# One projection unit moved among the indexer's products, and the search's first logits placed two units later

## Chip, cores and metric

The kernel runs on one core of a Trainium2 chip. The metric is the device time of one execution in microseconds (us). The engines are called PE (matrix products), DVE (vector), ACT (activation), POOL (GpSimd) and SP (the queue that issues nearly all DMAs here).

## What is computed

One layer over 2048 tokens of width 1024: a root-mean-square norm, one wide projection, two attention branches with gates, an output projection, and a last norm.

```python
xn = rms_norm(h, norm_gain[layer])
proj = xn @ w_in[layer]
qa, ka, va, ga, qb, kb, vb, gb, iq, ik, iw, za, zb = jnp.split(proj, offsets, axis=-1)
ya = chunked_relpos_attention(qa, ka, va, rel_bias[layer]) * jax.nn.silu(ga)
...
yb = dsa_sparse_attention(qb, kb, vb, iq, ik, iw) * jax.nn.silu(gb)
gate_a = jax.nn.sigmoid(za + b_merge[layer, 0])
gate_b = jax.nn.sigmoid(zb + b_merge[layer, 1])
merged = gate_a * (ya @ w_branch_a[layer]) + gate_b * (yb @ w_branch_b[layer])
h = h + merged @ w_out[layer]
```

`dsa_sparse_attention` first scores all admissible keys of a query with the small indexer (`iq`, `ik`, `iw`: eight heads of width 32), keeps the best 256, and attends to those only.

## The kernel before

Tokens are worked on in four groups of 512. Every fp32 product is done as three products of rounded halves (`mm3`, L212): high by high, high by low, low by high. A product of 128 output columns with one group is thus 24 matmuls of 128x512 (8 slices of the width by 3), into one PSUM bank.

**Stage 1, the indexer.** The groups come in the order 2, 3, 0, 1 (index `i` from 0 to 3). Each has three products of 128 columns, `chain(i, m)`. The columns hold the indexer's queries, its keys, its head weights, and the key of branch B. For the first two groups the norm's factor is applied after the product; for the last two (groups 0 and 1) `scaled(i)` applies it before: DVE multiplies eight slices in place (L230), ACT writes the high half `xh` (L231), DVE the low half `xl` (L232). The factor comes from `squares(i)` (sums of squares of rows, on ACT), `root_columns` (a chain of tiny DVE operations) and `root_rows` (four PE transposes into the bank `trr`, then an ACT copy, L305). `evac_i(i, m)` empties a bank: for `m = 0` through the rotary tables `cs` (loaded by DMA into one buffer) into `ea`; then ACT and DVE write a high and a low half into `e` (three buffers, L337 and L338) and SP sends them to DRAM as `iqD`, `ikD` and `kB`. After the second and the fourth group the keys come back in another layout as `ikT` (L348). `weights_t` transposes the head weights (`trw`).

**Stage 2, the projection.** The other columns stand in 20 units of 256 columns (`UNITS`; unit 0 is the first quarter of `zb`). `prep(u)` loads a unit's weights through staging tiles `wst` (SP), and splits them: ACT the high half (L209), POOL the low half (L210). There are two weight buffers `wt`. In stage 1 they hold the inputs `xw` and the indexer's weights `w01`, so that unit 0 can be prepared only when group 0 has been scaled, and unit 1 only when the last indexer product is done. The list `jobs` goes through the units, first for groups 0 and 1 (two jobs a unit, two products a job), later for groups 2 and 3. `evac` empties a bank; for `zb` ACT applies the sigmoid with the bias `bm` and SP stores the tile in `sBD`.

**The search** runs beside stage 2. `tick(x)` stands behind each product and calls `pump`, which takes as much work as `PUMP * x` allows from two threads: `logits()` (the indexer's scores, `lg`: eight matmuls for each piece of keys, from `iqT` and `ikT`) and `search()` (the thresholds, on DVE and ACT). From the 142nd tick on, when both threads have ended, the same ticks start stage 3, the attention.

The code's order is not the engines' order: a scheduler places each engine's instructions, in PE's queue too, by times of its own. Within an engine and within SP's queue the order is then fixed, and an instruction that waits holds up all behind it.

The lines on which the change and the prediction rest are these (the numbering of the profile).

Of the kernel before, what the change touches and what calls it, by code (L numbers as in the profile page):

```python
# [8 lines left out]
F32 = mybir.dt.float32  # L9
# [87 lines left out]
def block_kernel(ctx: ExitStack, tc: tile.TileContext, io, dbg=None):  # L97
# [91 lines left out]
    wcur = {}  # L189
    stage = [(wpool, 2, 2)]  # L190

    def prep(u, gate=None, at=None):
        if (at or u) in wcur:
            return
        wt = wpool.tile([128, 2, KT, WT], F32R, name="wt", tag="wt")
        if UNITS[u][0] == "va":
            st = stage[-1][0].tile([128, KT, 32], F32, name="wst", tag="wst", bufs=stage[-1][2])
            nc.sync.dma_start(st, io["wV"][UNITS[u][1]])
            nc.scalar.activation(wt[:, 0, :, 256:288], st, AF.Copy)
            nc.gpsimd.tensor_tensor(wt[:, 1, :, 256:288], st, f32(wt[:, 0, :, 256:288]), op=OP.subtract)  # L200
        for c in range(2):
            pl, n, bufs = stage[-1]
            for k in range(0, KT, n):
                st = pl.tile([128, n, 128], F32, name="wst", tag="wst", bufs=bufs)
                if gate is not None:
                    nc.gpsimd.tensor_copy(st[:, 0, 0:1], gate)
                nc.sync.dma_start(st, io["wP"][u, c, :, k:k + n, :])
                hi = wt[:, 0, k:k + n, c * 128:(c + 1) * 128]
                nc.scalar.activation(hi, st, AF.Copy)  # L209
                nc.gpsimd.tensor_tensor(wt[:, 1, k:k + n, c * 128:(c + 1) * 128], st, f32(hi), op=OP.subtract)  # L210
        wcur[at or u] = wt
# [22 lines left out]
    with ExitStack() as ph:  # L234
# [59 lines left out]
        def root_columns(i, n):  # L294
            v = xp.tile([128, 4 * n], F32, name="v4", tag=f"v{n}{i}")
            nc.vector.tensor_scalar(v, ss[:, 4 * i:4 * i + 4 * n], 1.0 / D, EPS, op0=OP.mult, op1=OP.add)
            r = rsqrt(xp, v, f"rs{n}{i}", 4 * n)
            for z in range(n):
                inv_[i + z] = r[:, 4 * z:4 * z + 4]

        def root_rows(i):
            tr = psl.tile([128, 512], F32, name="trr", tag="lg1")
            for j in range(4):
                nc.tensor.transpose(tr[:, j * 128:j * 128 + 128], inv_[i][:, j:j + 1].to_broadcast([128, 128]), ident)
            nc.scalar.activation(roots_[order[i]], tr, AF.Copy)  # L305
# [3 lines left out]
        def chain(i, m, c=all_):  # L309
            s_ = SLOT[order[i]]  # L310
            if (i, m) not in accs:
                n = rot("first", 7)
                accs[i, m] = (psp, psp, ps, ps, ps, psl, psl)[n].tile([128, 512], F32, name="xa",
                                                                       tag=f"acc{n}" if n < 5 else ("lg0", "ptr0")[n - 5])
            w_ = w_of(m)
            mm3(accs[i, m][:, c], [((w_[0][:, k], w_[1][:, k]), (xh[s_][:, k, c], xl[s_][:, k, c])) for k in range(KT)])
# [38 lines left out]
            nc.scalar.activation(iw[:, 4 * g:4 * g + 4, :], tr[:, :, 112:120], AF.Copy, scale=0.0625)  # L355

        nc.sync.dma_start(gcol, io["g1"])
        for k in range(0, KT, 2):
            load_x(0, k, k + 2, halves[0])
            load_w(0, k)  # L360
# [8 lines left out]
        def scaled(i):  # L369
            for k in range(KT):  # L370
                split_x(SLOT[order[i]], k, x32[i % 2][:, k], roots_[order[i]])

        def roots_of(i):
            root_columns(i, 1)
            root_rows(i)
# [18 lines left out]
        for m in range(3):  # L394
            chain(1, m)
        scaled(2)
        for m in range(3):
            evac_i(0, m)
        weights_t(0)
        for m in range(3):  # L400
            chain(2, m)
        squares(3)
        roots_of(3)
        squares(1)
        roots_of(1)
        scaled(3)
        prep(0)
        for m in range(3):
            evac_i(1, m)
        weights_t(1)  # L410
        for m in range(3):
            evac_i(2, m)
        for m in range(3):
            chain(3, m)
# [1 line left out]
        for m in range(3):  # L416
            evac_i(3, m)
        weights_t(3)


    ph = phase_p
    evl = search_st.enter_context(pool("evl", bufs=2, side="right"))
# [210 lines left out]
        nc.vector.tensor_scalar(gt, gt, -1.0, -FAR, op0=OP.add, op1=OP.mult)  # L633
        nc.gpsimd.dma_start(mskD[b, :, :n], gt)

    nc.sync.dma_start(bm, io["bm"])
    threads = {0: logits(), 1: search()}
    clock = {0: 0.0, 1: 0.0}

# [538 lines left out]

    def tick(x):
        due[1] += x  # L1180
        if threads:
            pump(PUMP * x)
        elif due[1] > OPEN:
            if not early_:
                open_early()
            due[0] += x * ROUNDS
            while due[0] >= 1 and not paused:
                due[0] -= 1
                if next(att_gen) == "late":
                    paused.append(1)  # L1190
# [13 lines left out]
    def next_acc(i):  # L1204
        n = rot("acc", 3 if 1 < i < ACC3 else 2)
        return (psp, psp, psz)[n].tile([128, 512], F32, name="acc", tag=f"acc{n}")
# [83 lines left out]
    for i, (how, r_, u, g) in enumerate(jobs):  # L1290
        kind, c2 = UNITS[u]
        wt, s_ = wcur[r_], SLOT[g]
        if how == "one":
            for n, _ in enumerate(first_half(u, wt)):
                if u == quads[-1] and n == 1:
                    for k in range(4):
                        combine_pe(A21, A22, A21, 1, k, 1)
                tick(0.5)
        for c in range(0 if how == "one" else 4 if kind == "va" else 2):
            acc = next_acc(i)  # L1300
            if kind == "va":
                c_ = slice(c * 128, c * 128 + 128)
                mm3(acc[:, :WT], [((xh[s_][:, k, c_], xl[s_][:, k, c_]), (wt[:, 0, k, :], wt[:, 1, k, :]))
                                  for k in range(KT)])
                evac_v(c2, g, c, acc[:, :WT])
                for _ in range(1):
                    if again:
                        again.pop(0)()
                tick(0.5)
            else:  # L1310
                w_ = slice(c * 128, c * 128 + 128)
                mm3(acc, [((wt[:, 0, k, w_], wt[:, 1, k, w_]), (xh[s_][:, k, :], xl[s_][:, k, :]))
                          for k in range(KT)])
                evac(kind, c2 * 2 + c, g, acc)
                for _ in range(2):
                    if again:
                        again.pop(0)()
                tick(1)
        if i in range(BI0, BI0 + 16):
            bias_half(i - BI0, f32(wt[:, 1, KT - 1, 255:256]))  # L1320
        if (u, g) in ((b_, 0), (b_, 1)) and r_ < nu:
            again += norm_again(g + 2)
        if i == turned:
            again += [lambda k=k: combine(A21, A11, A21, OP.subtract, k) for k in range(4)]
        for n in after.get(i, []):
            if n < nu:
                prep(n)
            elif n < 2 * nu:
                prep(n - nu, at=n)
            else:  # L1330
                while again:
                    again.pop(0)()
                prep_one(n - 2 * nu, n)
# [204 lines left out]
```

## Time and profile before

| what | value |
|---|---|
| median of three runs | 2072.44 us (2071.0 to 2077.87) |
| the profiled execution, its own time | 2072.23 us |
| its span, first to last instruction | 2070.4 us |
| PE busy | 1988.5 us, 96% of the span |
| DVE, ACT, POOL busy | 71%, 61%, 39% |
| mean granted PE clock | 0.991 |

A row of the timeline gives the start, the length, the engine, the line and the tiles (out<-in), the number of instructions merged, and in brackets how long the engine had been idle and what released it. Matmuls overlap, so a row's length is more than the distance to the next one. In the table of windows, each stretch has its length, each engine's busy time with the number of instructions, the granted PE clock and the DMA engines' share. Stage 1 reaches to about 100 us, stage 2 to about 1016 us.

### The profile page before, as it was taken

How to read it: one execution, taken by the hardware profiler on the slowest of the kernel's cores; microseconds unless marked ns; L12 is line 12 of the kernel's file. 1: busy time of each engine (PE TensorE's matmuls, PEld its weight loads, DVE VectorE, ACT ScalarE, POOL GpSimd, SP SyncE). 2: the span in 40 equal slices, each digit the busy share in tenths (PEclk: the TensorE clock that was granted, in tenths of full speed). 3: DMA queues.
4: the chain of work that ended last, by engine and by line, in shares of the span. 5: the costliest groups of instructions: out<-in, count | busy, mean ns of one | idle time of the engine just before them, and what ended most of it. 6: DMA issues, size and time to landing. Idle time of an engine off the chain costs nothing.

```text
span 2070.4 us, 34079 instructions
## 1 busy us (share of the span) xinstructions
PE 1988.5 (96%) x10674; PEld 1684.4 (81%) x10674; DVE 1472.0 (71%) x3646; ACT 1266.2 (61%) x2484; POOL 798.6 (39%) x1043
## 2 busy tenths in 40 slices
PE   8799999999999999999898999999999999999998
PEld 7588887889889887877677889888888888887786
DVE  6748887978789987474466768758886688765444
ACT  5456566556567554244587869858987688773221
POOL 2122233321132454444345464454444633432410
PEclk9899999999999999999999999999999999999999
DMA  9473345464464665578999775565355631335642
GB/s 359 143 236 129 120 133 161 129 207 143 172 193 138 217 212 188 186 238 286 285 308 275 210 234 153 169 221 160 120 168 166 219 114 52 99 94 179 214 137 92
DMA packets 262154, 375.75 MB, mean 181 GB/s; under 512 B 32080, under 2 KB 127696, under 8 KB 261840
## 3 DMA queue, kind: packets, MB, share of 16 engines
q1 hardware_dynamic: 261968, 373.53, 56.6%
q8 instruction: 85, 1.39, 0.3%
q14 instruction: 101, 0.83, 0.1%
HBM read 252.88 MB, written 120.55 MB: 180 GB/s over the span
## 4 chain that ended last, share of the span: by engine, by line
PE 43%; DMA 5%; DVE 3%; ACT 3%; issue 3%; POOL 2%; SPq 1%; DVEq 0%; POOLq 0%; ACTq 0%
PE d L218 7%; PE acc L218 6%; PE po L1433 6%; PE O L1016 5%; PE s L991 5%; PE pt L1008 4%; PE O L926 3%; PE s L881 2%; PE pt L916 2%; DMA mf<-mD 1%; DMA wst<-wS 1%; DVE P L812 1%; ACT P L994 1%; POOL dw L1055 1%; DMA bias<-biasD 0%
## 5 line engine op out<-in xcount | busy, mean ns | idle before, releaser
L218 PE MATMUL acc<-xh,wt 128*128 128x512 f32 x2160 | 696.8, 396 | 17.6 <-ACT wt L1250 7.8
L218 PEld LDWEIGHTS acc<-xh,wt 128*128 128x128 f32 x2160 | 405.3, 189 | 114.6 <-ACT wt L1250 11.0
L218 PE MATMUL acc<-xl,wt 128*128 128x512 f32 x1080 | 424.1, 393 | 0.0
L833 POOL TENSOR_TENSOR ptl<-pf,pth 128x512 fp32r<-128x512 f32 (+1 forms) x144 | 180.1, 1251 | 229.7 <-ACT pf L829 158.6
L218 PEld LDWEIGHTS acc<-xl,wt 128*128 128x128 f32 x1080 | 203.9, 189 | 43.0
L210 POOL TENSOR_TENSOR wt<-wst,wt 128x512 fp32r<-128x512 f32 (+1 forms) x92 | 118.2, 1312 | 271.5 <-ACT wt L209 239.6
L836 DVE TENSOR_TENSOR ptl<-pt,pth 128x512 fp32r<-128x512 f32 (+1 forms) x288 | 187.9, 660 | 43.6 <-ACT pth L835 42.0
L487 DVE SCALAR_TENSOR_TENSOR sc<-lg,iw,sc 128x512 f32<-128x512 f32 (+2 forms) x266 | 178.9, 679 | 42.4 <-ACT lg L482 37.2
L991 PE MATMUL s<-kBt,qsB 128*128 128x512 f32 (+3 forms) x640 | 187.1, 384 | 2.4 <-DVE mx L812 2.1
L482 ACT ACTIVATE lg<-lg 128x512 f32<-128x512 f32 (+2 forms) x304 | 149.4, 523 | 63.3 <-PE lg L480 61.9
L835 ACT ACTIVATE pth<-pt 128x512 fp32r<-128x512 f32 (+1 forms) x288 | 159.8, 579 | 26.2 <-PE pt L1008 16.0
L1008 PE MATMUL pt<-ident,P 128*128 128x128 f32 x1088 | 166.6, 273 | 1.0 <-DVE ptl L836 0.6
L994 ACT ACTIVATE P<-P,mx 128x128 f32<-128x128 f32 (+15 forms) x128 | 154.8, 1210 | 18.7 <-DVE mx L812 18.5
L1016 PE MATMUL O<-ptl,vBt 128*128 128x256 f32 x544 | 148.7, 299 | 2.7 <-POOL ptl L833 1.5
L1016 PE MATMUL O<-pth,vBt 128*128 128x256 f32 x544 | 147.6, 289 | 2.1 <-ACT pth L835 0.7
L812 DVE CUSTOM_DVE_ANT_0 P<-s,mk,mx 128x512 f32<-128x512 f32 (+2 forms) x192 | 125.2, 652 | 32.5 <-PE s L991 26.3
L1008 PEld LDWEIGHTS pt<-ident,P 128*128 128x128 f32 x1088 | 127.7, 140 | 9.0 <-DVE ptl L836 1.8
L1250 ACT ACTIVATE wt<-wst 128x512 fp32r<-128x512 f32 (+1 forms) x144 | 75.1, 570 | 86.7 <-POOL wst L1350 43.7
L1055 POOL TENSOR_TENSOR dw<-dst,dw 128x512 fp32r<-128x512 f32 x64 | 82.5, 1291 | 94.1 <-ACT dw L1054 86.8
L1251 DVE TENSOR_TENSOR wt<-wst,wt 128x512 fp32r<-128x512 f32 (+1 forms) x144 | 92.6, 675 | 32.6 <-ACT wt L1250 32.3
L991 PEld LDWEIGHTS s<-kBt,qsB 128*128 128x128 f32 x640 | 102.2, 190 | 14.9 <-DVE mx L812 8.1
L881 PE MATMUL s<-kk,qs 128*128 128x320 f32 (+1 forms) x448 | 107.0, 335 | 7.2 <-DVE mx L812 3.5
(274 smaller groups left out, 4442.2 us busy)
## 6 DMA issues: line engine op xcount, KB each, us to landing
wst<-wP SPq DMA_DIRECT2D x84, 256.0 KB
wst<-wS SPq DMA_DIRECT2D x72, 256.0 KB
qs<-qA SPq DMA_DIRECT2D x128, 128.0 KB
kk<-kA SPq DMA_DIRECT2D x56, 256.0 KB
vs<-vA SPq DMA_DIRECT2D x56, 256.0 KB
qD<-q SPq DMA_DIRECT2D x54, 256.0 KB
wst<-wS SPq DMA_DIRECT2D x72, 192.0 KB
part<-qD SPq DMA_DIRECT2D x54, 256.0 KB
```

What stands on the lines that cost most here:

```text
L218: nc.tensor.matmul(acc, a, b, start=(first and i == 0), stop=(last and i == n - 1), **({} if first and last else {"skip_group_check": True}))
L482: nc.scalar.activation(lg, lg, AF.Relu)
L487: nc.vector.scalar_tensor_tensor(o_, lg, wv, o_, op0=OP.mult, op1=OP.add)
L812: nc.vector.tensor_tensor_reduce(dst, ps_, add, 1.0, FMAX if first else mx, OP.add, OP.min, accum_out=mx)
L833: nc.gpsimd.tensor_tensor(lo, pf, f32(hi), op=OP.subtract)
L835: nc.scalar.activation(hi, src, AF.Copy)
L836: nc.vector.tensor_tensor(lo, src, f32(hi), op=OP.subtract)
L881: nc.tensor.matmul(s_ps[:, :w], q[:, m, j * 128:(j + 1) * 128], kk[:, ko:ko + w], start=(m == 0), stop=(m == 1))
L991: nc.tensor.matmul(s_ps[:, :w], q[:, h, :], kBt[:, m, a:a + w], start=(m == 0), stop=(m == 1))
L994: nc.scalar.activation(P[:, e, :n], P[:, e, :n], AF.Exp, bias=mx[:, e:e + 1], scale=-1.0, accum_out=st["sum"][:, (u % 2) * 2 + e:(u % 2) * ...
L1008: nc.tensor.transpose(pt[:, k, e, :], P[:, e, (kt + k) * 128:(kt + k + 1) * 128], ident)
L1016: nc.tensor.matmul(o_, vBt[:, kt + k, :], src[:, k, :], start=(kt + k == 0 and n_ == 0), stop=(kt + k == b and n_ == 1), skip_group_check= ...
```

## The change

Unit 0 for group 0 (two products, 48 matmuls) is taken out of the list of jobs and written into stage 1, with its own evacuation. Its weights are loaded right after group 0 is scaled, through the staging tiles of stage 1 (six buffers of 128 KB, in place of two), and its bias table `bm` at the very start. Group 0's products are written in another order, one of them is evacuated at once, and the counter that hands out banks skips one. The job that is left empty still ticks twice, and `tick` does nothing until its count is over 4, so that the first logits come after the fifth product's tick, where they came after the first's.

```diff
+    def prep(u, gate=None, at=None, via=None):
...
+            pl, n, bufs = via or stage[-1]
...
+                st = pl.tile([128, n, 128], F32, name="wst", tag="wis" if via else "wst", bufs=bufs)
...
         nc.sync.dma_start(gcol, io["g1"])
+        nc.sync.dma_start(bm, io["bm"])
...
         scaled(2)
+        prep(0, via=(xp, 2, 6))
         for m in range(3):
             evac_i(0, m)
         weights_t(0)
-        for m in range(3):
-            chain(2, m)
         squares(3)
-        roots_of(3)
+        root_columns(3, 1)
+        chain(2, 1)
+        chain(2, 0)
+        root_rows(3)
+        chain(2, 2)
+        evac_i(2, 1)
+        scaled(3)
+        for c in range(2):
+            acc = (ps, psl)[c].tile([128, 512], F32, name="xa", tag=("acc2", "ptr0")[c])
+            c_ = slice(c * 128, c * 128 + 128)
+            mm3(acc, [((wcur[0][:, 0, k, c_], wcur[0][:, 1, k, c_]), (xh[0][:, k], xl[0][:, k])) for k in range(KT)])
+            e = ev.tile([128, 512], F32, name="ef", tag="ef")
+            nc.scalar.activation(e, acc, AF.Sigmoid, bias=bm[:, 8 + c:9 + c])
+            nc.sync.dma_start(sBD[0][c_], e)
+        rot("first", 7)
         squares(1)
         roots_of(1)
-        scaled(3)
-        prep(0)
...
-        for m in range(3):
+        for m in (0, 2):
             evac_i(2, m)
...
-    nc.sync.dma_start(bm, io["bm"])
...
     def tick(x):
         due[1] += x
+        if due[1] <= 4:
+            return
...
+            if i == 0:
+                tick(1)
+                continue
```

Three places show how the scheduler places this. First, PE in stage 1, where the root factors of groups 3 and 1 are transposed (`rs13y`, `rs11y` belong to indices 3 and 1); `xh_142` to `xl_145` are group 0's halves, `xh_146` to `xl_149` those of the next group, `w_181` and `w_182` the indexer's weights, `wt` those of unit 0. Before:

```order
L218 MATMUL xa<-xh_144,w_181 128x512
L304 MATMUL trr<-ident,rs13y 128x128 x4
L304 MATMUL trr<-ident,rs11y 128x128 x4
L218 MATMUL xa<-xh_146,w_181 128x512
L218 MATMUL xa<-xh_146,w_182 128x512
```

Now:

```order
L218 MATMUL xa<-xh_144,w_181 128x512
L304 MATMUL trr<-ident,rs13y 128x128 x4
L218 MATMUL xa<-xh_142,wt 128x512 x2
L218 MATMUL xa<-xl_143,wt 128x512
L218 MATMUL xa<-xh_142,wt 128x512 x2
L218 MATMUL xa<-xl_143,wt 128x512
```

Between the two sets of transposes there now stand 43 of the 48 matmuls of unit 0 (the other five come 24 matmuls earlier), and behind them the transposes of `rs11y` and the last group's products.

Second, SP's queue from the last group's writes to the weights of unit 1 (`wst`). Before:

```order
L344 DMA ikD<-e 8x2x512
L344 DMA iqD<-e 32x2x512 x2
L344 DMA kB<-e 8x2x512 x2
L348 DMA ikT<-ikD 32x1024 x4
L344 DMA iqD<-e 128x2x512
L344 DMA iqD<-e 32x2x512 x2
L344 DMA kB<-e 48x2x512
L457 DMA iqT<-iqD 32x8x128 x4
L698 DMA sBD_94<-ef 128x512
L457 DMA iqT<-iqD 32x8x128 x4
L698 DMA sBD_94<-ef 128x512
L207 DMA wst<-wP 128x512 x5
```

Now:

```order
L708 DMA sBD_95<-ef 128x512
L344 DMA ikD<-e 24x2x512
L344 DMA ikD<-e 8x2x512
L344 DMA iqD<-e 32x2x512 x2
L344 DMA kB<-e 8x2x512 x2
L348 DMA ikT<-ikD 32x1024 x4
L344 DMA iqD<-e 128x2x512
L344 DMA iqD<-e 32x2x512 x2
L344 DMA kB<-e 48x2x512
L708 DMA sBD_95<-ef 128x512
L468 DMA iqT<-iqD 32x8x128 x2
L207 DMA wst<-wP 128x512 x5
```

Four loads of `iqT` went ahead of the last group's writes and two behind the weights; a store of the sigmoid's result (`sBD`, of unit 0 with group 1) now stands ahead of those writes.

Third, PE around the first logits (`lg`). Before, they stand inside the last product of unit 0:

```order
L218 MATMUL acc<-xh_146,wt 128x512
L218 MATMUL acc<-xl_147,wt 128x512
L218 MATMUL acc<-xh_146,wt 128x512 x2
L480 MATMUL lg<-ikT,iqT 128x384 x5
L218 MATMUL acc<-xl_147,wt 128x512
```

Now they stand between unit 0's last product and unit 1's first, all eight in a row:

```order
L354 MATMUL trw<-ident,ea 128x128 x4
L218 MATMUL acc<-xh_148,wt 128x512 x2
L218 MATMUL acc<-xl_149,wt 128x512
L218 MATMUL acc<-xh_148,wt 128x512
L491 MATMUL lg<-ikT,iqT 128x384 x8
L218 MATMUL acc<-xh_142,wt 128x512
L218 MATMUL acc<-xl_143,wt 128x512
```

The last 5294 of PE's 10676 instructions, from about 1172 us in the run before (the first products of branch B's output), stand in the same order in both kernels.

More of the change, by code (lines that the diff above doesn't have):

```diff
@@ L190, in block_kernel @@
     stage = [(wpool, 2, 2)]
-    def prep(u, gate=None, at=None):
+    def prep(u, gate=None, at=None, via=None):
         if (at or u) in wcur:
@@ L201, in prep @@
         for c in range(2):
-            pl, n, bufs = stage[-1]
+            pl, n, bufs = via or stage[-1]
             for k in range(0, KT, n):
-                st = pl.tile([128, n, 128], F32, name="wst", tag="wst", bufs=bufs)
+                st = pl.tile([128, n, 128], F32, name="wst", tag="wis" if via else "wst", bufs=bufs)
                 if gate is not None:
```

## The prediction, made before the changed kernel ran

> **What bounds the kernel now.** I read the page's busy times and slices first, then the table of windows, then PE's timeline for the first 130 us, since all that the change moves lies there.
>
> ```profile
> PE 1988.5 (96%) x10674; PEld 1684.4 (81%) x10674; DVE 1472.0 (71%) x3646; ACT 1266.2 (61%) x2484; POOL 798.6 (39%) x1043
> PE   8799999999999999999898999999999999999998
> ```
>
> PE is the bound: it is idle for 82 us of 2070.4, and the slices put much of it in the first two (52 us each). Both kernels give PE the same 10,676 matmuls, so a gain can only come from PE's idle time or its clock.
>
> ```profile
> 50.00:66.00 16.00, 12.85 (x61) 10.23 (x60) 11.43 (x39) 10.24 (x21) 4.55 (x5) 1.00 0.60 205
> 66.00:70.00 4.00, 0.98 (x5) 0.70 (x5) 2.67 (x6) 2.37 (x5) 2.18 (x3) 0.84 0.72 200
> 70.00:78.00 8.00, 1.05 (x2) 0.29 (x1) 7.97 (x9) 5.02 (x9) 4.10 (x3) 0.50 0.02 4
> 78.00:84.00 6.00, 5.60 (x17) 4.32 (x17) 5.94 (x10) 0.00 (x0) 0.00 (x0) 0.64 0.12 30
> 102.00:118.00 16.00, 16.00 (x72) 12.99 (x72) 2.39 (x4) 4.58 (x7) 0.00 (x0) 1.00 0.83 247
> 130.00:668.00 538.00, 534.05 (x2654) 453.68 (x2653) 450.41 (x1096) 323.50 (x640) 152.15 (x165) 1.00 0.48 156
> 668.00:1016.00 348.00, 332.30 (x1421) 265.73 (x1421) 240.84 (x470) 159.82 (x271) 161.13 (x313) 0.99 0.68 223
> ```
>
> The columns are length, then busy time and count for PE, its weight loads, DVE, ACT and POOL, then PE's clock. Between 66 and 78 us PE does almost nothing while DVE is full, and the clock falls to 0.50. The 102 to 118 row gives the price of a matmul at full clock: 72 in 16.00 us, four of them short transposes, so 0.23 us. From 130 to 668 us PE idles 4 us in all, from there to the attention 15.7 us.
>
> ```profile
> 53.70 0.50 PE L218 MATMUL xa<-xh,w 128*128 128x512 f32 x1 [1.41 <-DVE more L335]
> 67.81 0.65 PE L304 MATMUL trr<-ident,rs11y 128*128 128x128 f32 x4 [1.92 <-ACT work L305]
> 69.67 0.79 PE L218 MATMUL xa<-xh,w 128*128 128x512 f32 x1 [1.21 <-ACT xh L231]
> 77.41 0.80 PE L218 MATMUL xa<-xh,w 128*128 128x512 f32 x1 [6.95 <-DVE more L335]
> 78.61 0.79 PE L218 MATMUL xa<-xl,w 128*128 128x512 f32 x1 [0.40 <-DVE xl L232]
> 81.76 0.91 PE L218 MATMUL xa<-xh,w 128*128 128x512 f32 x2
> 100.79 0.50 PE L218 MATMUL acc<-xh,wt 128*128 128x512 f32 x1 [3.15 <-DVE e L338]
> 118.94 1.04 PE L480 MATMUL lg<-ikT,iqT 128*128 128x384 f32 x5
> 124.23 0.63 PE L218 MATMUL acc<-xh,wt 128*128 128x512 f32 x2
> 125.18 0.44 PE L480 MATMUL lg<-ikT,iqT 128*128 128x384 f32 x1
> ```
>
> The waits that the change can reach are 1.92 + 1.21 + 6.95 + 0.40 + 3.15 = 13.6 us. PE's clock is half from the restart at 77.41 to about 82.4: 5 us at half speed, 2.5 us lost. Sum on offer: 16.1 us. The second matmul of the row at 124.23 is unit 1's first, at 124.46; five logits stand before it. I use that moment as the mark: all later work is the same, so the result is the shift of the mark, corrected for what is done before it.
>
> **Where stage 1 ends now.** Two small moves first. The load of `bm` goes ahead of the first inputs, one issue of SP: 0.4 us later. The transposes of group 0's root stand six matmuls earlier in PE's queue: 6 x 0.23 = 1.4 us earlier. The small DVE chain behind them meets POOL's splits of unit 0's weights sooner, and ACT takes three more of those splits ahead of the roots; I let these cancel and start from 53.70 as before.
>
> ```profile
> 0.74 0.39 SPq L357 DMA_DIRECT2D gcol<-g  x1
> 38.40 5.39 DVE L230 SCALAR_TENSOR_TENSOR xw<-xw,gcol,work 128x512 f32<-128x512 f32 x8 [7.65 <-ACT work L305]
> 67.78 8.85 DVE L230 SCALAR_TENSOR_TENSOR x<-x,gcol,work 128x512 f32<-128x512 f32 x8 [1.27 <-ACT work L305]
> 71.79 2.31 POOL L210 TENSOR_TENSOR wt<-wst,wt 128x256 fp32r<-128x256 f32 x2
> 69.22 2.61 POOL L327 TENSOR_TENSOR cs<-cs,roots 128x1024 f32<-128x1024 f32 x1 [0.81 <-POOL wt L210]
> 68.49 0.60 ACT L305 ACTIVATE roots<-trr 128x512 f32<-128x512 f32 x1 [0.74 <-PE trr L304]
> 77.87 1.89 DVE L232 TENSOR_TENSOR xl<-x,xh 128x512 fp32r<-128x512 f32 x3
> ```
>
> PE from 53.70: 24 + 5 + 24 matmuls (12.2 us) and four transposes (0.4) to 66.3, index 3's transposes to 66.9, ACT's copy to 67.5. Then DVE scales the last group. This took 5.39 us for group 0 and 8.85 for the last, where POOL was at work beside it; now POOL has nothing to do there (its splits are done, and its table waits for the other root), so 5.4, to 73.0. The low halves, 8 x 0.63, take DVE to 78.0. PE meanwhile has unit 0: 43 x 0.23 = 9.9 us, to 76.8, so its 48 matmuls lie fully in the old hole. Then the transposes of `rs11y` (77.4) and ACT's copy (78.0). What is late next is the bank: DVE's first emptying of group 1's sums, 0.65 us behind that copy and the low halves, at 78.7. PE idles 1.3 us, too short for the clock to fall. The rest of stage 1 and unit 0 with group 1 are 120 matmuls (27.6) and three sets of transposes (1.1): PE is through at 107.4, where the old order needs until 124.4. The wait of 3.15 goes, since the next bank is that of the product emptied first.
>
> **What comes next is not ready.** PE now meets the eight logits and unit 1, and both hang on SP's queue.
>
> ```profile
> 85.53 0.63 ACT L337 ACTIVATE e<-ea 128x512 fp32r<-128x512 f32 x1 [8.24 <-DVE ea L332]
> 95.01 0.63 ACT L337 ACTIVATE e<-ea 128x512 fp32r<-128x512 f32 x1 [4.26 <-DMA kB<-e]
> 99.42 0.60 ACT L337 ACTIVATE e<-xa 128x512 fp32r<-128x512 f32 x1 [3.77 <-DMA iqD<-e]
> 103.41 0.63 ACT L337 ACTIVATE e<-ea 128x512 fp32r<-128x512 f32 x1 [1.74 <-DMA kB<-e]
> 104.80 0.64 SPq L344 DMA_DIRECT2D ikD<-e  x2
> 107.85 1.70 SPq L348 DMA_DIRECT2D ikT<-ikD  x4
> 111.95 2.84 SPq L457 DMA_DIRECT2D iqT<-iqD  x4
> 115.53 2.51 SPq L457 DMA_DIRECT2D iqT<-iqD  x4
> 118.78 3.28 SPq L207 DMA_DIRECT2D wst<-wP  x5
> 123.46 0.63 ACT L209 ACTIVATE wt<-wst 128x512 fp32r<-128x512 f32 x1 [4.50 <-DMA wst<-wP]
> 124.17 2.55 POOL L210 TENSOR_TENSOR wt<-wst,wt 128x512 fp32r<-128x512 f32 x2 [50.07 <-ACT wt L209]
> ```
>
> The writes of `e` pass on at the pace of three buffers that wait for DMAs to land (85.53, 95.01, 99.42, 103.41). None of this gets shorter. Group 1's `ea` is ready at 83.2 (78.0, the table's 2.61, four DVE operations of 0.65), 2 us earlier, but the last group's first `e` now waits in ACT's queue behind the sigmoid of unit 0 with group 1: PE ends that product at 78.7 + 96 x 0.23 + 0.8 = 101.6, the sigmoid at 102.4. It also waits for the one `cs` buffer: its load stands behind index 2's last writes, at about 97, and lands some 4.3 later like the DMAs above, and 2.6 of DVE follow. So 104 to 105 instead of 103.41, and `ikD` goes out near 105.7 (105 to 107), 0.9 later than at 104.80.
>
> From `ikD` to the weights SP took 118.78 - 104.80 = 14.0 us. Six loads of `iqT` fewer (0.71 and 0.63 each) and one store less (about 0.5) save 4.5. But the two loads of `iqT` left there read what the last `iqD` writes, which must land first. `ikT` waited until 107.85 for an `ikD` issued by 105.44, 2.4 us; ACT's waits of 4.26 and 3.77 are the upper bound. This gives back 1 to 3, so 11.5 (10 to 13): the weights are issued near 117.2 and ready 5.3 us later (118.78 to 124.09), at 122.5. Bounds: 120.3 with the early ends, 125.3 with the late ones. The logits wait for `ikT`, issued from about 108.5, and are done by 117 or so: not the last.
>
> **The sum.** The mark moves from 124.46 to 122.5: 2.0 us gained, and three logits more are behind it (0.5). PE idles from 107.4 but for the logits, as from 66 to 77, so unit 1 starts at half clock: 2.3 lost (0 if the logits keep the clock up, 2.5 as at 77.41). Net 0.2 us: of 16.1 us filled, all but that returns as one wait ahead of unit 1. The profiled execution's span becomes 2070.2, its own time 2072.0; that execution lies 0.2 below the median of the runs shown, so I say 2072. The ends of this part alone: ready at 120.3 at full clock gains 4.7, at 125.3 and half clock loses 2.8.
>
> On the clock, the Trainium skill ("TensorE: Matmul & The Clock Gate", section on what is happening) says that one idle window of about 3.4 us halves it and about 3.4 us of sustained work restores it. The trace shows the fall to 0.50 and took 5 us to restore. By the page's figure the loss would be an estimated 1.7, and the sum 0.6 us lower.
>
> **Behind the mark.** Stage 2 is placed anew by the scheduler, with the search 4 ticks later.
>
> ```profile
> L582 PE MATMUL lg<-ones,bad x2: 163/164/165, 819.2 to 819.2; 128*1 128x1 f32 x2
> L881 PE MATMUL s<-kk,qs x448: 219/310/522, 1016.7 to 1743.9; 128*128 128x320 f32 x128, 128*128 128x128 f32 x6, 128*128 128x512 f32 x6, 128*128 128x256 f32 x5
> PE lg L480 <- DVE sc L487: 3.3, 3, 1.4
> ```
>
> The search ends at 819.2 and is first needed when the attention starts at 1016.7: 197 us of room for a delay of some 25 us (four products with their logits). Cost nothing; if it were gone, the attention's start would be next. PE waits for DVE's scores 3.3 us in three places. A new order can take these away or add as many: 4 us either way.
>
> **Rivals.**
>
> *The hole is filled for good.* If unit 1's weights were there when PE is through, at 107.4 + 1.4 for the logits, PE would gain 16.1 - 1.3 = 14.8: 2057. Against it stands SP's queue, which has the weights behind the last group's writes. It is measurable, 6.2 us, only if the weights go out near 111, 5 us after `ikD`, or if half the gain of the early bound meets a luckier stage 2. 14%.
>
> *The later search costs PE.* DVE is busy 450 of 538 us beside the units, and the search's last 25 us move behind 819, among the units whose weight halves DVE itself splits. If PE's waits from 668 to 1016 (15.7 in 348) become twice as dense from 819 on, that is 197 / 348 x 15.7 = 8.9 us more: 2081. It decides from 6.2 us on, a 40% rise of those 15.7 us. For it speaks that PE idles just there; against it, that DVE is at 69% there (240.84 of 348) and PE idles only 4 us where DVE is at 84%. 17%.
>
> *The hole isn't reached*, because unit 0's weights come late. Even with two staging buffers their last splits ended at 74.1 (POOL's row at 71.79), and PE now needs these in the product that begins at 71.3: at most 2 us, and six buffers bring them sooner. No chance of its own.
>
> **How the numbers follow.** No change, 2072 by the terms above with 4 us either way for stage 2: 69%. The range must leave out at most 2 in 10, and takes in the phase bounds (-4.7, +2.8) and part of both rivals: 2065 to 2079. 0.3%, 6.2 us, is about what a measurement here can tell from no change. Faster 14%, same 69%, slower 17%.
>
> **What would show it.** Right: no PE gap over 2 us between 54 and 105; L230 for the last group near 5.4 us; PE idle most of 107 to 122, in two parts around eight logits, the second ended by ACT's or POOL's split of unit 1; a granted clock of 0.5 there. Wrong: unit 1's weights issued before 112, or PE's idle from 130 to 1016 away from 20 us by more than 5.

## The result, and the profile after

The changed kernel takes 2088.09 us (median of six runs, 2085.12 to 2091.48) against 2072.68 for the kernel before (six runs): a ratio of 1.0064, 95% interval 1.0053 to 1.0076. It is slower by some 13 to 15 us. The forecast was no change, 2072, with a range of 2065 to 2079. The profiled execution has a span of 2087.6 us and a time of 2089.46.

The page of the changed kernel, busy times and the slices of PE:

```profile
PE 1998.8 (96%) x10674; PEld 1692.9 (81%) x10674; DVE 1467.8 (70%) x3646; ACT 1264.1 (61%) x2482; POOL 789.0 (38%) x1043
PE   8989999999999999988897999999999999999998
```

PE does the same matmuls, yet is busy for 10.3 us longer than before (1998.8 against 1988.5): some of them ran at half clock. Its idle time grew by 6.9 us only (88.8 against 81.9). The slices show where: slices 18 to 22, about 890 to 1150 us, went from 9 9 8 9 8 to 8 8 8 9 7. In the second and third, where the change was made, 7 9 became 9 8.

The windows of the changed kernel, in the columns of the prediction's table:

```profile
50.00:66.00 16.00, 11.63 (x42) 9.08 (x42) 12.49 (x36) 11.13 (x24) 7.34 (x9) 0.79 0.75 264
66.00:78.00 12.00, 12.00 (x55) 9.77 (x55) 7.45 (x16) 6.34 (x10) 0.00 (x0) 1.00 0.31 91
107.00:130.00 23.00, 14.47 (x48) 10.52 (x47) 9.79 (x16) 9.92 (x23) 4.71 (x4) 0.70 0.77 223
668.00:1016.00 348.00, 330.37 (x1411) 264.85 (x1409) 247.08 (x492) 163.83 (x278) 150.81 (x305) 0.99 0.65 215
```

The old hole from 66 to 78 us is full: PE 12.00 of 12 at full clock, where it had 2.03. Instead there is a new hole between 107 and 130 us, 8.5 us idle at a mean clock of 0.70.

Timeline of the changed kernel up to unit 1 (PE, then one row of DVE and two of SP's queue):

```profile
53.18 0.62 PE L304 MATMUL trr<-ident,rs10y 128*128 128x128 f32 x4 [2.95 <-DVE rs10y L150]
55.22 0.79 PE L218 MATMUL xa<-xh,w 128*128 128x512 f32 x1 [1.41 <-DVE more L335]
83.24 0.50 PE L218 MATMUL xa<-xh,w 128*128 128x512 f32 x1 [1.55 <-DVE more L335]
118.06 4.00 PE L491 MATMUL lg<-ikT,iqT 128*128 128x384 f32 x8 [5.50 <-DMA ikT<-ikD]
125.03 0.80 PE L218 MATMUL acc<-xh,wt 128*128 128x512 f32 x1 [2.96 <-ACT wt L209]
...
71.95 5.39 DVE L230 SCALAR_TENSOR_TENSOR x<-x,gcol,work 128x512 f32<-128x512 f32 x8 [4.28 <-ACT work L305]
...
111.62 0.65 SPq L344 DMA_DIRECT2D ikD<-e  x2
121.27 2.49 SPq L207 DMA_DIRECT2D wst<-wP  x5
```

Unit 1 starts at 125.03, against 124.46 before: nothing gained, as forecast. So the loss must lie behind. Three landmarks that both kernels pass show where: the first combination of halves of the input (`cm`), the first product of branch A's output (`d<-ya`), the first of branch B's (`d<-yb`). The number to read is the first start, ahead of "to". Kernel before:

```profile
L1241 PE MATMUL cm<-xh,unit x16: 393/398/592, 870.0 to 894.3; 128*128 128x512 f32 x16
L218 PE MATMUL d<-ya,dw x384: 388/394/628, 1078.4 to 1818.2; 128*128 128x512 f32 x192
L218 PE MATMUL d<-yb,dw x384: 387/390/507, 1172.3 to 1962.5; 128*128 128x512 f32 x192
```

Changed kernel:

```profile
L1253 PE MATMUL cm<-xh,unit x16: 393/399/500, 872.2 to 895.4; 128*128 128x512 f32 x16
L218 PE MATMUL d<-ya,dw x384: 388/396/505, 1091.2 to 1835.8; 128*128 128x512 f32 x192
L218 PE MATMUL d<-yb,dw x384: 387/390/503, 1190.3 to 1979.7; 128*128 128x512 f32 x192
```

It trails by 2.2 us at 870, by 12.8 at 1078 and by 18.0 at 1172; from there the two run alike, and the span ends 17.2 later. Nearly 16 us of this are lost some 750 us behind the place of the change, in two stretches: the partial products (`part`, the units that are computed from sums and differences of blocks) and the start of the attention. Windows over them, before and then after:

```profile
900.00:1020.00 120.00, 112.13 (x479) 88.13 (x477) 64.29 (x110) 52.84 (x92) 48.98 (x97) 1.00 0.87 281
1020.00:1130.00 110.00, 95.84 (x521) 79.37 (x521) 70.29 (x202) 93.41 (x222) 50.87 (x65) 0.97 0.98 299
```

```profile
900.00:1020.00 120.00, 107.28 (x445) 84.45 (x444) 62.41 (x103) 50.39 (x89) 48.78 (x98) 0.97 0.80 259
1020.00:1130.00 110.00, 91.73 (x463) 75.19 (x462) 62.38 (x172) 78.74 (x182) 40.33 (x52) 0.92 0.98 287
```

From 900 to 1020 PE gets through 34 matmuls fewer (445 against 479). From the first landmark to the second, before and then after:

```profile
870.00:1078.40 208.40, 189.21 (x826) 149.42 (x824) 124.44 (x226) 114.94 (x210) 84.33 (x146) 0.98 0.83 273
```

```profile
872.20:1091.20 219.00, 194.67 (x840) 154.99 (x838) 127.49 (x227) 114.14 (x215) 84.87 (x147) 0.95 0.80 258
```

Of the 10.6 us between these, 5.1 are longer idle time and 5.5 longer busy time. The landmarks cut the work at slightly different places: 13 small matmuls of the attention (four `s`, nine `pt`) stand ahead of `d<-ya` now and stood behind it before. So the split of a loss between the two stretches is good to 1 or 2 us only; the sum of both is firmer.

### The profile page after: what moved, and what is told of

Its sections match the earlier page's. It is cut to its first block, busy times and chain, and to the rows that moved or that the text cites. A ratio compares the mean times of both kernels' runs of the same rounds, so it can differ in the third digit from the quotient of the medians.

```text
span 2087.6 us, 34087 instructions
## 1 busy us (share of the span) xinstructions
PE 1998.8 (96%) x10674; PEld 1692.9 (81%) x10674; DVE 1467.8 (70%) x3646; ACT 1264.1 (61%) x2482; POOL 789.0 (38%) x1043
## 4 chain that ended last, share of the span: by engine, by line
PE 70%; DMA 10%; DVE 8%; issue 5%; ACT 4%; POOL 2%; SPq 2%; DVEq 0%; ACTq 0%; POOLq 0%
PE acc L218 27%; PE d L218 8%; PE po L1448 6%; PE O L1026 6%; PE s L1001 5%; PE pt L1018 5%; PE O L936 3%; PE s L891 3%; PE pt L926 3%; PE lg L491 2%; PE xa L218 2%; DMA wst<-wS 2%; DMA mf<-mD 1%; DVE P L822 1%; DMA sBD<-part 1%
## 5 line engine op out<-in xcount | busy, mean ns | idle before, releaser
L218 PE MATMUL acc<-xh,wt 128*128 128x512 f32 x2128 | 691.3, 398 | 20.1 <-ACT wt L1262 12.8
L491 PE MATMUL lg<-ikT,iqT 128*128 128x512 f32 (+2 forms) x304 | 104.5, 377 | 10.2 <-DMA ikT<-ikD 5.5
```

The costliest lines, as they stand in the source:

```text
L218: nc.tensor.matmul(acc, a, b, start=(first and i == 0), stop=(last and i == n - 1), **({} if first and last else {"skip_group_check": True}))
L491: nc.tensor.matmul(lg[:, :w], iqT[:, h, :], ikT[:, c0:c0 + w], start=True, stop=True)
```

## What the wait for weights looks like

One of the new waits, followed back through the changed kernel's timeline. SP issues all loads and stores in a fixed order; `part<-qD` loads sums, `sBD<-part` stores a result from the same buffers, `wst<-wS` loads the next weights, POOL combines them, ACT splits them, PE multiplies:

```profile
937.30 4.56 SPq L1372 DMA_DIRECT2D part<-qD  x2
941.95 0.38 SPq L708 DMA_DIRECT2D sBD<-part  x1
945.08 0.32 SPq L1372 DMA_DIRECT2D part<-qD  x1
945.45 0.90 SPq L1363 DMA_DIRECT2D wst<-wS  x2
...
948.49 0.45 POOL L1364 TENSOR_TENSOR wst<-wst 128x128 f32<-128x128 f32 x1 [10.73 <-DMA wst<-wS]
...
949.50 0.52 ACT L1262 ACTIVATE wt<-wst 128x384 fp32r<-128x384 f32 x1 [5.93 <-POOL wst L1365]
...
950.08 0.50 PE L218 MATMUL acc<-xh,wt 128*128 128x512 f32 x1 [3.33 <-ACT wt L1262]
988.85 0.50 PE L218 MATMUL acc<-xh,wt 128*128 128x512 f32 x1 [3.08 <-ACT wt L1262]
1017.89 0.50 PE L218 MATMUL acc<-xh,wt 128*128 128x512 f32 x1 [2.40 <-ACT wt L1262]
```

SP issues a store at 941.95 and then nothing until 945.08: the load of sums next in its queue waits for a buffer, and the weights behind it wait too, though DVE's last split of the weights before them was over at 941.6. What the loads of sums wait for, from 941 to 946.5 us (total, number, longest), is that an earlier result from the same buffer has landed:

```profile
SPq L1372 <- DMA qB<-part: 3.9, 1, 3.9
SPq L1372 <- DMA sBD<-part: 2.7, 1, 2.7
```

In the kernel before the same load of weights goes out at this time:

```profile
935.88 0.44 SPq L1348 DMA_DIRECT2D wst<-wS  x1
```

It is 9.6 us earlier. What stands between two such groups of weights in SP's queue differs. Before, and then now:

```
L1348 DMA wst_9399<-wS 128x384
L1357 DMA part<-qD_124 128x512
L719 DMA qB_74<-eh 128x512
L719 DMA qB_74<-part 128x512
L1357 DMA part<-qD_110 128x512
L1348 DMA wst_9461<-wS 128x384
```

```
L1363 DMA wst_9399<-wS 128x384
L708 DMA sBD_97<-part 128x512
L1372 DMA part<-qD_110 128x512
L729 DMA qB_75<-eh 128x512
L729 DMA qB_75<-part 128x512
L1372 DMA part<-qD_124 128x512
L1372 DMA part<-qD_111 128x512
L708 DMA sBD_97<-part 128x512
L1372 DMA part<-qD_124 128x512
L1363 DMA wst_9461<-wS 128x384
```

Two loads of sums stood ahead of these weights, now four do. The code of this phase is the same in both kernels; the scheduler has placed it in another order. I call them the first and the second order. The first has one wait of 3.26 us for weights (at 1008.72) and smaller ones; the second has the three above. Each of the three is followed by a stretch at half clock, here the first of them and what comes behind it, and the two others; the last row belongs to the attention's start, behind a wait of 3.69 us:

```profile
951.90:955.30 3.40, 3.40 (x9) 2.66 (x9) 2.44 (x5) 2.18 (x4) 2.17 (x5) 0.51 1.00 321
955.30:958.70 3.40, 3.40 (x16) 2.79 (x16) 1.90 (x3) 0.53 (x1) 0.90 (x3) 0.99 0.90 285
989.50:992.90 3.40, 3.40 (x9) 2.49 (x9) 2.09 (x4) 2.08 (x4) 2.53 (x6) 0.50 0.68 224
1020.20:1023.60 3.40, 3.40 (x9) 2.64 (x8) 1.62 (x3) 1.57 (x3) 0.73 (x2) 0.50 0.84 269
1037.30:1044.10 6.80, 5.99 (x18) 4.91 (x19) 4.22 (x13) 6.77 (x18) 3.65 (x8) 0.50 1.00 330
```

Nine matmuls in 3.40 us instead of sixteen: 7 x 0.23 = 1.6 us a time. Waits and clock together come to 8.8 + 4.8 = 13.6, less the first order's 3.26 + 1.26 + 1.12 = 5.6, so 8 of the 10.6 us by which the lag grows from 870 to 1078. This is a rough sum: the first order, too, has a stretch at half clock there, 1021.0 to 1024.4, which it leaves out.

The attention's start has several orders too: that of the kernel before, that of the changed kernel, and a third that two of the runs below have. One edit matters for which it is: the job that is left empty skips two calls of `next_acc`, which deals out three accumulator banks in turn, so that all later products use other banks than before.

## The experiments

Theories. Q: the orders of the late phase cost the time, whatever stands in stage 1. S: the search, which ends later (its last test on PE starts at 826.8 instead of 819.2), costs it. M: the moved products themselves cost it. The table gives ratios to the kernel before as run on the same chip, and the lag of the profiled execution behind the kernel before at the three landmarks. "-" where the landmark itself was moved.

| run | stage 1 | hold, ticks | partial products | attention's start | ratio (95% interval) | lag at `cm`, `d<-ya`, `d<-yb`, us |
|---|---|---|---|---|---|---|
| changed kernel | new | 4 | second | changed kernel's | 1.0064 (1.0053 to 1.0076) | 2.2, 12.8, 18.0 |
| e1_wait1 | new | 1 | first | changed kernel's | 1.0031 (1.0017 to 1.0044) | 1.0, 2.4, 8.6 |
| e2_before_wait2 | old | 2 | second | third | 1.0103 (1.0083 to 1.0122) | 7.0, 14.9, 19.1 |
| e3_before_wait4 | old | 4 | first | before's | 1.0024 (1.0014 to 1.0034) | -1.2, 3.5, 3.4 |
| e4_no_wait | new | 0 | second | changed kernel's | 1.0095 (1.0077 to 1.0112) | 3.6, 14.4, 18.9 |
| e5_rot_wait1 | new | 1 | first | before's | 1.0007 (0.9996 to 1.0018) | -4.0, -3.0, -1.3 |
| e6_rot | new | 4 | second | third | 1.0063 (1.0044 to 1.0082) | 1.7, 8.8, 13.5 |
| e7_own | new | 4 | new buffers | of its own | 0.9993 (0.9980 to 1.0006) | -0.4, -1.0, 1.0 |
| e8_weights_early | new, unit 1's weights early | 5 | first | before's | 0.9969 (0.9959 to 0.9979) | -6.8, -5.3, -3.5 |
| e9_before_own | old | 0 | new buffers | of its own | 0.9992 (0.9981 to 1.0003) | -0.3, -, 1.4 |
| e10_both | as e8 | 5 | new buffers | of its own | 0.9948 (0.9932 to 0.9965) | -9.4, -, -6.2 |
| e11_both_attention_early | as e8 | 5 | new buffers | 8 ticks earlier | 1.0026 (1.0015 to 1.0037) | -10.9, -, 5.6 |

**One tick of hold instead of four.**

```diff
-        if due[1] <= 4:
+        if due[1] <= 1:
```

> The changed kernel with the search held back by one tick of the planner instead of four. Stage 1 is the changed one, matmul by matmul, up to unit 1. From the partial products (about 890 us) to 1170 us every engine's order is that of the kernel before, not that of the changed one. Theory Q, the order of the queues between 890 and 1170 us costs the 15 us: 2073.5 us (2072.7 of before plus the 0.9 by which the changed kernel trails at 237 us), 2070 to 2077. Theory S, the later search costs it: a quarter of the delay, a quarter of 15, 2076.5. Theory M, the moved products cost it: 2088.

Ratio 1.0031, 2079.71 us. This is between Q and M, and the reason is an error in the expectation: only the partial products have the order of the kernel before; the attention's start has that of the changed kernel. The lags say so too: 1.4 us are lost from 870 to 1078, where the changed kernel loses 10.6, and 6.2 from 1078 to 1172, where it loses 5.2. M falls, since nearly all of its loss in the first stretch is gone with the products still moved.

**The kernel before with a hold of two ticks, and of four.** Both put two lines into `tick`, and nothing else:

```diff
         due[1] += x
+        if due[1] <= 2:
+            return
```

> The kernel before with one line added: the search is held back by two ticks of the planner. Unit 0 stays where it was. From the partial products on, every engine's order is that of the changed kernel. Q: 2088, 2084 to 2091, the full loss without the moved products. S: half the delay, half the loss, 2080. M: 2072.7.

> The kernel before with the search held back by four ticks as in the changed kernel. Unit 0 stays where it was. From the end of the search on, every engine's order is that of the kernel before. Q: 2072.7, 2070 to 2076. S: the full loss, 2088. M: 2072.7.

Two ticks: 1.0103, 2092.05 us, as slow as the changed kernel or slower, with stage 1 untouched; it has the second order (though a third for the attention's start, where I had expected the changed kernel's). Four ticks, the hold of the change: 1.0024. S would have the longer hold cost more; it costs a quarter. So S falls as the main cause, and M again. But the search's end may not be free: of the 19.1 us of the run with two ticks, 7.0 are lost ahead of the partial products, where neither order of the late phase can be the reason (the changed kernel has 2.2 there). PE's longest wait there is 3.1 us for DVE, at 832.9, just behind the end of the search; that the search causes it is not shown. Nor is 1.0024 nothing: with every engine's order as before from the end of the search on, this kernel lost 4.7 us between 870 and 1078. PE was idle 2.2 us longer there and busy 2.5 us longer, at a mean clock of 0.96 where the kernel before has 0.98. Why the same order met longer waits is open.

**No hold at all.**

```diff
-        if due[1] <= 4:
-            return
```

> The changed kernel without the hold on the search; the moved products stay. From the end of the search on, every engine's order is that of the changed kernel. Q: 2088, 2084 to 2091. S: no loss, 2073.5. M: 2088.

1.0095, 2090.67 us: Q. The search isn't held back, and the loss is there in full.

**The banks dealt out as before, with one tick of hold.** This gives the moved products the late orders of the kernel before, all of them:

```diff
             if i == 0:
+                rot("acc", 2)
                 tick(1)
...
-        if due[1] <= 4:
+        if due[1] <= 1:
```

> The changed kernel with the search held back by one tick, and with unit 0's two skipped turns of the accumulator banks counted all the same. Stage 1 is the changed one; from the partial products on, every engine's order is that of the kernel before, the attention's start included. Theory Q in its narrower form (the second order of the partial products costs 9 to 10 us, the second order of the attention's start 6 to 7): both are gone, 2074, 2071 to 2077. If the moved products or the skipped turns cost time by themselves: 2080 like the run with one tick, or more.

1.0007 (0.9996 to 1.0018): no change. This is the run that answers the prediction. With the late phase in its old order, the moved products and the changed stage 1 are worth nothing either way, which is what was forecast for them. From the first landmark to the third, the four profiled executions with the order of the kernel before (that kernel, four ticks, this run, and the one with early weights below) take 302.3 to 306.9 us; the four with the second order of the partial products take 314.1 to 318.1. So one order alone varies by some 5 us, and the two orders lie apart beyond that. This run's window over the partial products:

```profile
900.00:1020.00 120.00, 110.34 (x464) 87.82 (x463) 60.22 (x105) 52.11 (x94) 45.20 (x93) 0.97 0.87 278
```

**The banks dealt out as before, hold of four ticks.** The first of the two edits alone.

> The changed kernel with its hold of four ticks, and the two skipped turns of the accumulator banks counted. The partial products keep the second order; the attention's start takes the order that it had in the kernel before with a hold of two ticks, where it lost nothing. Narrow Q: 2088 less 6 to 7, so 2082, 2079 to 2085. If the attention's start loses time whatever its order (because it comes late): 2088.

1.0063 (1.0044 to 1.0082) is the changed kernel's ratio, and my expectation would be 1.0045, at the very edge. The third order of the attention's start loses 4.7 us from 1078 to 1172, and in the run with two ticks 4.2: it doesn't lose nothing, as I had thought from that run, but about what the changed kernel's order loses there (5.2, 6.2 and 4.5 in the three runs that have it). The order of the kernel before loses -0.1, 1.7 and 1.8. What within these orders costs the 4 to 6 us is open; in the changed kernel PE's longest wait there is for one of the attention's loads (`kk<-kA`, 3.9 us).

**Results of the partial products from buffers of their own.** Then a load of sums needs no earlier store to have landed:

```diff
-        evac(kind, c2 * 2 + (z > 0), 2 if z == 2 else 3, f32(s), own=s)
+        evac(kind, c2 * 2 + (z > 0), 2 if z == 2 else 3, f32(s))
```

> The changed kernel; the results of the partial products go out from buffers of their own, not from the buffer of the sums. A load of sums then waits for no store to land. If the loss in the partial products is that weight loads stand on SP behind loads of sums that wait for such a store: PE's three waits of 2.4 to 3.3 us between 945 and 1020 us go with their half clock, 3 x 4.8 = 14 us less, of which the kernel before had one too: 2074 to 2080. If the loads are late for the DMA engines' load (0.8 busy there), the waits stay: 2086 to 2090. If the new buffers (two of each kind) make ACT wait instead: 2088 or more.

0.9993, 2073.83 us: the whole loss is gone. PE's wait for these weights between 900 and 1020 us, in total, number and longest, in the changed kernel and with the edit:

```profile
PE acc L218 <- ACT wt L1262: 12.2, 7, 3.3
```

```profile
PE acc L218 <- ACT wt L1262: 0.4, 1, 0.4
```

and the window with the edit:

```profile
900.00:1020.00 120.00, 117.26 (x503) 94.58 (x504) 66.51 (x118) 58.70 (x108) 53.42 (x104) 0.97 0.92 311
```

That the DMA engines were simply too busy is out: they now move more in the same time (311 GB/s against 259), and the weights come. SP's own waits agree. From 880 to 1020 us its loads of sums wait for a store to land for 31.8 to 34.9 us in the five executions with the first order, for 40.3 to 42.3 in the four with the second, and with the edit only once, for 0.3; PE's wait for weights from 900 to 1020 goes with it, at 6.3 to 8.3, 9.3 to 12.2 and 0.4 us. So the weights were late because of what stood ahead of them on SP. The edit also gives another order, so it doesn't show how much of the gain is the freed buffer alone.

**Unit 1's weights called for early.** Behind `weights_t(2)`, through the staging tiles of stage 1; the banks as before; a hold of five ticks:

```diff
         weights_t(2)
+        prep(1, via=(xp, 2, 6))
         for m in range(3):
             evac_i(3, m)
...
             if i == 0:
+                rot("acc", 2)
                 tick(1)
...
-        if due[1] <= 4:
+        if due[1] <= 5:
```

> The changed kernel with unit 1's weights called for ahead of the last group's writes, through the staging buffers of the projection's weights; banks' turns counted, hold of five ticks, by which the first logits stand behind 54 of unit 1's products and the orders from the partial products on are those of the kernel before. If the 11.4 us won by 118 us were lost only because unit 1's weights and the logits came late: PE goes on at 108 us, and 2073 + 1 - 12 = 2062, 2059 to 2067. If the early loads hold up the last group's writes on SP: the logits come later still, and 2070 to 2076.

0.9969 (0.9959 to 0.9979): 2069.77 us, faster by 6.4 by the ratio. Where the changed kernel has its new hole, this one's window reads so, and its last split of the early weights on ACT:

```profile
102.00:130.00 28.00, 28.00 (x125) 22.59 (x124) 4.74 (x7) 6.88 (x14) 5.24 (x6) 1.00 0.74 200
103.81 0.42 ACT L209 ACTIVATE wt<-wst 128x256 fp32r<-128x256 f32 x1 [0.55 <-DMA wst<-wP]
```

PE doesn't stop, and the hole is filled for good. The size came out at the low end of the range: 6.4 us, where the sum had 2073 - 2062 = 11. Of the gain, 6.8 us are left at 870 and 3.5 at 1172 in the profiled execution.

**The kernel before with buffers of its own, and both edits together.**

> The kernel before; the results of the partial products go out from buffers of their own. It too had one wait of 3.3 us for weights (1008.7 us) and three of about 1.2. If those waits are what can be won: ratio to before 0.996 to 0.998 (4 to 8 us). If the attention's first products after 1020 us are limited by the DMA engines, which are 0.97 busy there in both kernels, the gain is there at 1020 us and given back by 1110: ratio 0.999 to 1.000.

> The changed kernel with unit 1's weights called for early (as in the run that did only this) and with buffers of their own for the partial products' results. From the partial products on PE's order is that of the kernel before with such buffers. If the gains add: 0.9969 less what the own buffers bring to the kernel before, 0.993 to 0.997. If a limit by the DMA engines between 1020 and 1110 us takes the second gain: 0.997, as with the early weights alone.

The kernel before gains nothing (0.9992), though PE's waits for weights fall there too, from 6.3 to 1.6 us: the gain is gone again by `d<-yb`. Both together bring 0.9948 (0.9932 to 0.9965), 2065.71 us, the fastest version, 11.4 us under the kernel before on that chip. Its windows:

```profile
900.00:1020.00 120.00, 115.78 (x516) 93.03 (x515) 67.86 (x124) 64.67 (x120) 53.12 (x104) 1.00 0.95 317
1020.00:1130.00 110.00, 94.23 (x487) 78.89 (x486) 63.70 (x183) 83.03 (x196) 46.93 (x56) 0.89 0.90 263
```

By 1020 us it is far ahead; from 1020 to 1130 it does less than the kernel before (487 matmuls against 521, clock 0.89). The DMA engines aren't full there (0.90), so a limit by them, which I had offered, isn't shown. What limits the attention's start stays open.

**The attention let in eight ticks earlier**, on top of both edits:

```diff
-OPEN = 142
+OPEN = 134
```

> As the run before it, with the attention's first products let in eight ticks earlier (134 instead of 142), so that their loads start some 18 us sooner. If the DMA engines' load after 1020 us is the limit, spreading it over a stretch where they are 0.9 busy helps little: 0.995 to 0.998. If it was the order around the attention's start that gave gains back: below 0.995. If the loads now collide with those of the weights: above 0.998.

1.0026: 0.8% slower than without. PE's longest wait between 1010 and 1130 us is, by the profile, for ACT's split of branch A's output weights (`dw`), and ACT in turn waited for their load:

```profile
PE d L218 <- ACT dw L1065: 6.6, 1, 6.6
1104.90 0.63 ACT L1065 ACTIVATE dw<-dst 128x512 fp32r<-128x512 f32 x1 [5.29 <-DMA dst<-wA]
```

SP issued this load at 1100.01, behind loads of the attention (`qsB`, `sgB`). Of the three readings only the collision is left, and this wait fits it: a load of weights late among the attention's loads. It is one wait of 6.6 us, not the whole difference, and no run tests it alone. Letting the attention in eight ticks earlier, with the new order that this gives, costs some 16 us (2081.59 against 2065.71).

## Why the prediction was wrong, point by point

**Stage 1.** Right in kind. The hole was filled as described: L230 took 5.39 us for the last group (forecast 5.4), the wait for the bank was 1.55 us (1.3), no wait over 2 us between 55.3 and 105. Late by some 5 us: PE was through at 112.5 instead of 107.4. The forecast started "from 53.70 as before"; instead PE's first matmul came 1.06 us later (0.4 forecast for the load of `bm`), and the wait for `rs10y` ahead of that point grew from 1.62 us, the row of the kernel before, to 2.95:

```profile
51.66 0.62 PE L304 MATMUL trr<-ident,rs10y 128*128 128x128 f32 x4 [1.62 <-DVE rs10y L150]
```

So 55.22 stands in place of 53.70, 1.5 us later. Behind it the clock fell, which was not in the sum, as the first of these rows of the changed kernel shows: 5.88 us of matmuls at half clock, some 3 us lost.

```profile
54.20:61.10 6.90, 5.88 (x14) 4.63 (x15) 5.30 (x14) 4.91 (x11) 3.08 (x2) 0.51 0.52 179
115.70:129.30 13.60, 8.21 (x18) 5.74 (x19) 5.05 (x9) 6.70 (x16) 4.01 (x4) 0.50 0.93 277
```

**Unit 1's weights.** Issued at 121.27 (forecast 117.2), since `ikD` went out at 111.62 (105.7, bounds 105 to 107). The first matmul came at 125.03 (122.5, bounds 120.3 to 125.3). From `ikD` to the weights SP took 9.7 us, not 11.5. The half clock behind the hole was there (second row above): unit 1 ran at it from 125.03 to 129.3, some 2.1 us lost, against 2.3 forecast. The net of stage 1 was near zero: 0.9 us lost in the changed kernel at about 237 us, and no change in the run with the old late orders.

**The search.** It was held back by far less than the 25 us assumed (7.6), and it does not explain the loss: the run with no hold has the loss in full, and the one with the same four ticks in the kernel before has little of it. "Cost nothing" may be too strong all the same, since with two ticks 7.0 us are lost ahead of 877 us.

**Behind the mark.** This is the step that failed: "all later work is the same", then "A new order can take these away or add as many: 4 us either way". The term measured 15 to 16 us (15.8 from 870 to 1172 in the profiled execution). It was sized by PE's waits for DVE's scores (3.3 us in three places), the wrong wait. What the runs showed in its place is weights late in SP's queue, behind loads of sums that wait for stores, with the half clock that follows, and an attention's start that is 4 to 6 us longer in the new order. The rows shown had PE idle for 15.7 us from 668 to 1016, and the kernel before already waited 6.3 us for weights between 900 and 1020; and the search for losses ended at 1016.7, where the attention starts. The work was the same, its order was not: the front of the document gives the tail that is common to both kernels from about 1172 us on, and everything ahead of it was free to move. The test that I named, PE's idle time from 130 to 1016 away from 20 us by more than 5, did not fire at 23.6 (538 - 532.04 and 348 - 330.37): half clock doesn't count as idle time, and the 100 us behind 1016 were not in it. The other sign, unit 1's weights before 112, did not fire either.

**The rival with the later search** (2081) had the right sign and came near the stretch, but by the wrong mechanism. **The hole filled for good** was rightly held unlikely for this change, and for the stated reason: once the weights don't stand behind the last group's writes, PE goes on. That run gains 6.4 us, not the rival's 14.8.

## What to carry to other kernels

Where a scheduler places the code, a change at one end can re-deal the order at the other; compare the orders of all engines to the end, and price every stretch that differs by the waits that one queue can cause there, not by the waits that happen to be largest now. A loss far from the edit calls for the control that makes the same loss without the edit, and for the one that keeps the edit and restores the order. And where loads, stores and reloads of one buffer share a queue with a critical load, give the stores a buffer of their own: here the two kernels with that edit, in two different orders, came out at 0.9993 and 0.9992.

## What had not been expected of the hardware

Gaps of PE shorter than 3.4 us can cost clock: PE's gaps of 3.33, 3.08 and 2.40 us were each followed by 3.4 us at 0.50 to 0.51, setting in 1.8, 0.7 and 2.3 us after PE had started again. The starts lie on one raster: from 951.9 to 989.5, 1020.2 and 1037.3 us there are 11, 20 and 25 steps of 3.41 us. The kernel before had a gap of 3.26 us at 1008.72 and kept its clock until 1021.0. Both this gap and the one at 950.08 lie across two steps of the raster of their execution. Here is the emptier of the two steps, before and then now:

```profile
1003.90:1007.30 3.40, 1.56 (x7) 0.94 (x5) 0.69 (x1) 0.56 (x2) 0.17 (x1) 1.00 0.73 232
```

```profile
948.50:951.90 3.40, 1.46 (x4) 0.71 (x5) 1.54 (x3) 1.05 (x2) 2.80 (x6) 1.00 0.98 348
```

PE was idle for 1.84 us of this step before, and the clock stayed; it was idle for 1.94 us now, and the clock fell at its end. Ahead of the fall at 1020.2, 1.46 us idle in one step were enough. So the idle time within one step goes with the fall, not the length of a gap, but no sharp bound shows. Counted over such steps at full clock from 800 to 1130 us in all thirteen profiled executions, none with less than 1.3 us idle was followed by half clock, and every one with more than 2 us was; between these both occur. The Trainium skill ("TensorE: Matmul & The Clock Gate", section "What's actually happening") has a free-running activity window of about 3.4 us and one idle window as the price of the clock. The raster and the 3.4 us agree; that a whole window must be idle does not, since PE was busy for 1.46 of the 3.40 us ahead of the fall at 951.9.
